# A float32 decoder trunk: where the later sums of one w_down tile are made, and one more unit in seven products

## The chip, the cores and the metric

The kernel runs on one core of one Trainium2 chip. The metric is the time of one execution on the device, in microseconds (us). Three runs of the kernel before gave 2436.99, 2437.06 and 2437.28 us; the median is 2437.06 us. The profile is of one further execution, whose own time is 2436.77 us. In it the span from the first to the last instruction is 2435.1 us.

## The reference

Two layers over 256 positions and 2048 channels, all in float32:

```
h = rms_norm(x, mix_norm[l]);  proj = h @ w_in[l]          # q, k, v, u, v of the SGU, two gates
branch_a = sliding_window_attention(q, k, v, sinks) @ w_attn_branch[l]
branch_b = chunked_sgu(gelu(uv), ...) @ w_sgu_branch[l]
merged   = sigmoid(gate_a) * branch_a + sigmoid(gate_b) * branch_b
x  = x + merged @ w_out[l]
h2 = rms_norm(x, ffn_norm[l])
x  = x + (silu(h2 @ w_gate[l]) * (h2 @ w_up[l])) @ w_down[l]   # hidden width 5632
```

The matrix products are nearly all of the work. The inner width of the feed-forward part is 11 blocks of 512.

## The kernel before, in words

**Jobs.** The program is a list of jobs (`add_job`). Each job is one matrix product: 256 positions by K inputs, times K by 1024 outputs (512 for one job of keys and values). K is cut into *units* of 512 inputs. The outputs of a job lie in PSUM banks of 128 positions by 512 outputs.

**Three matmuls for one.** A float32 matrix is split into a high part in the float32r format and the remainder, the low part. Each block product is then three matmuls with 512 columns (`three`, lines 401 to 403): high by high, high input by low weight, low input by high weight. The weights' high parts `whi` are made by ACT (line 258) and their low parts `wlo` by DVE (line 266). Both work on a *part*, 128 x 1024 numbers.

**Whole steps and products.** A unit is done in one of two ways. In the plain way it takes four *whole steps*; each uses one part and issues 12 matmuls. In the other way (`m` of the job counts the units done so) the 2 x 2 blocks of the unit are multiplied in seven *products* after Winograd's form of Strassen's method. Each product uses one part and issues 6 matmuls, so the unit takes 42 matmuls and not 48. For that, four sums of weight blocks are made by DVE (`Stream.add`, line 242), with three parts more to split, and the four sums of the input blocks must exist too. The first seven to nine products of a job follow each other without a whole step between them.

**The stream.** `Stream.fill` runs ahead of TensorE: at step s it emits the high part of step s+5, the low part of step s+4 and the weight sums that are due. `SUM_AT` gives the due step of each sum, counted from the job's first product: for `m=1` they lie 6 to 3 steps ahead of it, for `m=2` 7 ahead to 1 behind. There are five buffers for low parts, so the low part of step s+4 can be written only when step s-1 is done on TensorE. The raw weights lie in five buffers of 1 MB that the queue of SP fills.

**The input side.** A `Unit` holds 512 inputs of all positions, transposed: the high part `uh` and the low part `ul`, and, if its products need them, the sums' high and low parts `sh` and `sl`. `transposed` makes a unit: DVE transposes blocks, POOL's queue gathers them by 16 small transfers, ACT splits off the high part and DVE the low part (line 592, or line 510 in `combine`). With `sums=True` it goes on to the sums in the same go: four additions of 128 x 256 (line 522), the split by ACT (line 525) and the low part by DVE (line 510). `add_sums` makes the same sums afterwards for a unit that already exists: it first adds high and low parts again (line 605) into a tile `full`, then does the same three things.

**The order.** Every engine executes in the order in which the program emits its instructions. `after(n, fn)` emits `fn` n slots later; a whole step is one slot and a product half a slot. DVE and ACT work off everything in one row: the parts of the stream, the evictions of finished banks, the input side.

**Places in memory.** The tiles `uh`, `ul`, `sh`, `sl`, the gates, the hidden blocks, the tiles of the transposition and the sums all come from one pool of 25 places (`N_BIG`). A tile gets a place with its first write. Where none is free, the writing instruction waits until the last reader of an older tile is done, and what stands behind it on its engine waits too.

**The stretches around the change.** In the token mixer the last jobs are, in this order: the first pair of the second branch's gates, the two jobs of the first branch (2 units each, no products; `branch(ga, 0)`, then `branch(ga, 2)`), the last pair of the second branch's gates (`gate(gb, 2)`, 4 units), and the two jobs of the second branch. The feed-forward part goes in rounds over the blocks 0-3, 4-7 and 8-10. A round has gate and up jobs for two blocks at a time, with two units in seven products, and then two w_down jobs. `M_DOWN` is `((1, 2), (1, 2), (1, 1))`: in the first two rounds the first w_down job has one unit in products, and the second has two. So block fs[1] of those rounds is the "second input tile" of w_down, whose sums only the second job uses.

Of the kernel before, what the change touches and what calls it, by code (L numbers as in the profile page):

```python
# [45 lines left out]
M_OUT, M_FFN, M_DOWN = (0, 1), (2, 2, 2), ((1, 2), (1, 2), (1, 1))  # L46
UP_TWO = (0, 2, 4, 6, 8)
M_Q = 0
M_GATE, M_ATT, M_SGU = (1, 1, 1, 1), (0, 0), (1, 0)
M_V, M_U = 1, 1  # L50
SGU_SUMS = 8


@with_exitstack
def hybrid_trunk(ctx: ExitStack, tc: tile.TileContext, x, mix_norm, w_in, q_norm, k_norm, sinks,
# [37 lines left out]
    NF = FF // CW  # L93
# [16 lines left out]
    sums, uses = {}, []  # L110
# [186 lines left out]
    def after(n, fn):  # L297
        steps.append((slot_no[0] + n, fn))
# [16 lines left out]
    def evicting(c, fn, then=None, ahead=None, late_then=THEN_LATE):  # L315

        if c == 0 or job_no[0] == len(jobs):
            for t in range(NT):
                if ahead is not None:
                    ahead(t)  # L320
                soon(lambda t=t: fn(t))
            if then is not None:
                after(1, then)
        else:
            late = behind(1, *T1_LATE)
            if ahead is not None:
                ahead(0)
                after(late - 1, lambda: ahead(1))
            soon(lambda: fn(0))
            after(late, lambda: fn(1))  # L330
            if then is not None:
                after(behind(2, *late_then), then)
# [200 lines left out]
    def transposed(units, c, src, cols=None, on_pe=False, sums=False, at_once=False):  # L533

        unit = Unit(sums)

        def scaled(k):
            return 1.0 if cols is None else cols[:, k:k + 1]

        def highs(k0, n, src_t):  # L540
            step = n if cols is None else 1
            for k in range(0, n, step):
                nc.scalar.activation(unit.hi[:, k0 + k:k0 + k + step, :], src_t[:, k:k + step, :], AF.Copy,
                                     scale=scaled(k0 + k))

        def lows(k0, n, src_t):
            step = n if cols is None else 1
            for k in range(0, n, step):
                kk = slice(k0 + k, k0 + k + step)
                nc.vector.scalar_tensor_tensor(  # L550
                    out=flat(unit.lo[:, kk, :]), in0=flat(src_t[:, k:k + step, :]), scalar=scaled(k0 + k),
                    in1=flat(unit.hi[:, kk, :].bitcast(F32)), op0=ALU.mult, op1=ALU.subtract)

        def ready():
            units[c] = unit

        if on_pe:
            pts = []
            for b in range(2):
                pt = ps_at.tile([P, 2, S], F32, tag="at", name=nm("pt"))  # L560
                for kk in range(2):
                    k = 2 * b + kk
                    for t in range(NT):
                        nc.tensor.transpose(pt[:, kk, t * P:(t + 1) * P], src[:, t, k * P:(k + 1) * P], ident)
                highs(2 * b, 2, pt)
                pts.append(pt)

            def rest():
                for b in range(2):
                    lows(2 * b, 2, pts[b])  # L570
                ready()

            if at_once:
                rest()
            else:
                after(1, rest)
            return

        tt = landed()
        n = gathered(tt, src)  # L580
        tv = tt.rearrange("p i k t c -> p (k t) i c")
        def scale_all():
            if cols is not None:
                for k in range(4):
                    nc.scalar.activation(tt[:, :, k], tt[:, :, k], AF.Copy, scale=scaled(k))

        def split():
            scale_all()
            nc.scalar.activation(blocks(unit.hi), tv, AF.Copy)

        def lower():
            nc.vector.tensor_tensor(out=blocks(unit.lo), in0=tv, in1=blocks(unit.hi).bitcast(F32), op=ALU.subtract)
            ready()

        if not sums:
            after(n, split)
            after(n + 1, lower)
        else:
            after(n, scale_all)
            combine(unit, tv, n + (cols is not None), ready)  # L600
# [423 lines left out]
    for l in range(DEPTH):  # L1024

        pl = layer[l]
        parameters(pl)
        kv = slot([P, NT, CW], name="kv")
        qs = [slot([P, NT, CW], name="q") for _ in range(2)]
        att, spa = Attention(pl), Spatial(pl, norm)  # L1030

        def scaled_into(c, dst, ps):
            evicting(c, lambda t: None,
                     ahead=lambda t: nc.scalar.activation(dst[:, t, :], ps[t], AF.Copy, scale=norm.r[t]))

        def kv_done(c, ps):
            scaled_into(0, kv, ps)
            att.keys(kv)
            if l:
                att.begin()  # L1040

        def q_done(c, ps):
            scaled_into(c, qs[c], ps)
            att.queries(c, qs[c])
            if c == 1 and not l:
                att.begin()

        after(2, lambda unit=norm.units[0]: add_sums(unit))
        for done in (kv_done, q_done)[::-1 if l else 1]:
            run(norm.units, done)  # L1050
        run(norm.units, spa.v)
        run(norm.units, spa.u)

        ga, gb, mT = [None] * NCH, [None] * NCH, [None] * NCH

        def gate(dst, j):
            def done(c, ps):
                dst[j + c] = slot([P, NT, CW], name="gate")
                def tanh(t):
                    nc.scalar.activation(dst[j + c][:, t, :], ps[t], AF.Tanh, scale=norm.rh[t])  # L1060

                evicting(c, lambda t: None, ahead=tanh)
            run(norm.units, done)

        def branch(dst, j, units, then=None):
            def done(c, ps):
                d = dst[j + c]

                def then_():
                    then(j + c)  # L1070
                    transposed(mT, j + c, ga[j + c], sums=j + c == 0)

                evicting(c, lambda t: nc.vector.scalar_tensor_tensor(out=d[:, t, :], in0=d[:, t, :], scalar=1.0,  # L1073
                                                                     in1=ps[t], op0=ALU.add, op1=ALU.mult),
                         then_ if then is not None else None)
            run(units, done)

        def merge(j):
            nc.vector.tensor_tensor(out=flat(ga[j]), in0=flat(ga[j]), in1=flat(gb[j]), op=ALU.add)

        for j in (0, 2):
            gate(ga, j)
        gate(gb, 0)
        for j in (0, 2):
            branch(ga, j, att.attT)
        after(SGU_SUMS, lambda unit=spa.sguT[0]: add_sums(unit))
        gate(gb, 2)
        for j in (0, 2):
            branch(gb, j, spa.sguT, merge)

        norm = Norm(ffn_cols(l))
        residual(mT, norm, max(M_FFN), scale=0.5)

        nxt = Norm(mix_cols(l + 1)) if l + 1 < DEPTH else None
        for i, fs in enumerate(ROUNDS):
            hid, hT = {}, {}

            def gate_done(f, c, ps):
                hid[f] = a = slot([P, NT, CW], name="hid")

                evicting(c, lambda t: None,
                         ahead=lambda t: nc.scalar.activation(a[:, t, :], ps[t], AF.Silu, scale=norm.r[t]))

            def up_done(f, c, ps):
                a = hid[f]

                def upped(t):
                    nc.vector.scalar_tensor_tensor(out=a[:, t, :], in0=ps[t], scalar=norm.r[t], in1=a[:, t, :],
                                                   op0=ALU.mult, op1=ALU.mult)

                evicting(c, upped, lambda: transposed(hT, f, a, on_pe=f == NF - 1, sums=f in fs[:max(M_DOWN[i])]))

            for f in fs[::2]:
                if f + 1 < NF:
                    run(norm.units, lambda c, ps: gate_done(f + c, c, ps))
                    run(norm.units, lambda c, ps: up_done(f + c, c, ps))
                else:
                    run(norm.units, lambda c, ps: (gate_done, up_done)[c](f, c, ps))
            if i == len(ROUNDS) - 1:
                if nxt is not None:  # L1120
                    prepare(l + 1)
                residual(hT, nxt, M_Q, out if nxt is None else None)
            else:
                partial(hT)
        norm = nxt
# [37 lines left out]
```

## Time and profile before

| what | value |
|---|---|
| median of three runs | 2437.06 us |
| the profiled execution's own time | 2436.77 us |
| its span | 2435.1 us |
| TensorE (PE) busy | 2419.4 us, 99% |
| weight loads (PEld) busy | 1992.8 us, 82% |
| VectorE (DVE) busy | 2080.6 us, 85% |
| ScalarE (ACT) busy | 1488.6 us, 61% |
| GpSimd (POOL) busy | 494.2 us, 20% |
| DMA | 530.81 MB, mean 218 GB/s |

Times in rows are microseconds from the start of the span, if not marked ns. A row of a timeline gives start, duration, engine, line of the kernel, operation, the tiles written and read, the shape of the tile and how many instructions are merged into the row; in brackets stand how long the engine was idle before it and what ended the wait. A row of the stretches gives the stretch, its length, then busy time and instruction count of each engine, the granted TensorE clock, the busy share of the DMA engines and GB/s. Matmuls are pipelined and the ends of their rows are modelled, so they overlap: the distance of two starts is what a matmul costs. The count of an engine in a stretch includes what reaches in from the neighbouring stretch.

### The profile page before, as it was taken

What the parts mean: (1) busy time and instruction counts of PE and PEld (TensorE: products, weight loads), DVE (VectorE), ACT (ScalarE), POOL (GpSimd) and SP (SyncE); (2) the same over time, 40 slices, a digit from 0 to 9 for tenths busy, and PEclk for the clock granted to TensorE, in tenths of its full rate; (3) what the DMA queues carried; (4) which work ended last, traced back from release to release, by engine and by line L of the source; (5) the groups of instructions that cost most, each with busy time, mean ns of one, the idle gap of its engine ahead of it and who ended that gap; (6) DMA issues with size and microseconds to landing.
All of it is one profiled execution on the core that took longest, in us unless ns stands there. A gap on an engine that the chain in (4) does not pass through costs nothing.

```text
span 2435.1 us, 30941 instructions
## 1 busy us (share of the span) xinstructions
PE 2419.4 (99%) x10866; PEld 1992.8 (82%) x10866; DVE 2080.6 (85%) x2271; ACT 1488.6 (61%) x1828; POOL 494.2 (20%) x919
## 2 busy tenths in 40 slices
PE   9999999999999999999999999999999999999999
PEld 7888888888888887888888888888887888788887
DVE  7898768788988899889879977687789888988896
ACT  6566546466666666575666655554667566656663
POOL 1421300541220022002235123004402200220020
PEclk9999999999999999999999999999999999999999
DMA  8655556776576657666776555567855766476664
GB/s 309 202 191 186 180 180 223 227 261 227 185 259 199 245 196 242 211 223 225 263 248 230 193 169 189 185 207 220 291 209 192 257 188 258 162 268 189 250 209 171
DMA packets 174701, 530.81 MB, mean 218 GB/s; under 512 B 23617, under 2 KB 26289, under 8 KB 174545
## 3 DMA queue, kind: packets, MB, share of 16 engines
q1 hardware_dynamic: 142128, 491.73, 58.3%
q0 software_dynamic: 32096, 36.83, 5.9%
q8 instruction: 85, 1.39, 0.2%
q14 instruction: 72, 0.58, 0.1%
q10 hardware_dynamic: 320, 0.27, 0.0%
HBM read 483.66 MB, written 16.78 MB: 206 GB/s over the span
## 4 chain that ended last, share of the span: by engine, by line
PE 93%; DVE 3%; ACT 2%; DMA 1%; issue 1%; POOL 0%; DVEq 0%; ACTq 0%
PE acc L401 30%; PE acc L402 30%; PE acc L403 30%; DVE wlo L266 1%; ACT whi L258 1%; DMA tt<-blk 1%; PE po L891 1%; PE psc L849 1%; DVE sum L242 1%; PE ppt L880 0%; DMA raw<-in_w_in_dram 0%; PE psg L958 0%; DVE sums L522 0%; ACT acc L437 0%; DVE raw L242 0%
## 5 line engine op out<-in xcount | busy, mean ns | idle before, releaser
L266 DVE TENSOR_TENSOR wlo<-raw,whi 128x1024 fp32r<-128x1024 f32 (+1 forms) x970 | 1161.2, 1220 | 252.0 <-PE acc L402 145.3
L258 ACT ACTIVATE whi<-raw 128x1024 fp32r<-128x1024 f32 (+1 forms) x970 | 1007.9, 1056 | 569.7 <-PE acc L403 486.7
L401 PE MATMUL acc<-whi,uh 128*128 128x512 f32 x2864 | 1121.5, 392 | 1.9 <-DVE gate L1073 1.5
L402 PE MATMUL acc<-wlo,uh 128*128 128x512 f32 x2864 | 1115.2, 389 | 3.4 <-DVE wlo L266 3.4
L403 PE MATMUL acc<-whi,ul 128*128 128x512 f32 x2864 | 1115.1, 389 | 0.3 <-DVE ul L550 0.2
L491 POOL DMA_DIRECT2D tt<-blk x800 | 392.3, 498 | 1388.2 <-issue 331.2
L401 PEld LDWEIGHTS acc<-whi,uh 128*128 128x128 f32 x2864 | 537.6, 188 | 116.8 <-issue 2.3
L402 PEld LDWEIGHTS acc<-wlo,uh 128*128 128x128 f32 x2864 | 537.7, 188 | 115.6 <-DVE wlo L266 5.8
L403 PEld LDWEIGHTS acc<-whi,ul 128*128 128x128 f32 x2864 | 537.6, 188 | 113.7 <-DVE ul L550 0.6
L258 ACT ACTIVATE whi<-sum 128x1024 fp32r<-128x1024 f32 x144 | 152.4, 1058 | 123.9 <-PE acc L403 103.3
L402 PE MATMUL acc<-wlo,sh 128*128 128x512 f32 x576 | 224.9, 390 | 1.8 <-DVE wlo L266 1.8
L401 PE MATMUL acc<-whi,sh 128*128 128x512 f32 x576 | 225.4, 391 | 0.9 <-ACT acc L437 0.5
L403 PE MATMUL acc<-whi,sl 128*128 128x512 f32 x576 | 224.3, 389 | 0.0
L266 DVE TENSOR_TENSOR wlo<-sum,whi 128x1024 fp32r<-128x1024 f32 x144 | 175.1, 1219 | 19.6 <-PE acc L402 18.1
L401 PEld LDWEIGHTS acc<-whi,sh 128*128 128x128 f32 x576 | 108.1, 188 | 27.4 <-ACT acc L437 5.4
L402 PEld LDWEIGHTS acc<-wlo,sh 128*128 128x128 f32 x576 | 108.1, 188 | 26.5 <-DVE wlo L266 4.2
L403 PEld LDWEIGHTS acc<-whi,sl 128*128 128x128 f32 x576 | 108.1, 188 | 22.5
L437 ACT ACTIVATE acc<-acc 128x512 f32<-128x512 f32 x144 | 84.6, 587 | 23.2 <-PE acc L403 21.9
L242 DVE TENSOR_TENSOR raw<-raw,sum 128x1024 f32<-128x1024 f32 x72 | 88.2, 1225 | 2.5
L242 DVE TENSOR_TENSOR sum<-raw 128x1024 f32<-128x1024 f32 x72 | 87.9, 1220 | 1.9 <-DMA raw<-in_w_gate_dram 1.5
L242 DVE TENSOR_TENSOR sum<-raw,raw 128x1024 f32<-128x1024 f32 x72 | 88.0, 1222 | 0.8
L242 DVE TENSOR_TENSOR raw<-raw,raw 128x1024 f32<-128x1024 f32 x72 | 87.8, 1220 | 0.6 <-DMA raw<-in_w_gate_dram 0.5
(128 smaller groups left out, 1050.7 us busy)
## 6 DMA issues: line engine op xcount, KB each, us to landing
raw<-in_w_in_dram SPq DMA_DIRECT2D x112, 1024.0 KB, 5.5
raw<-in_w_down_dram SPq DMA_DIRECT2D x88, 1024.0 KB, 7.0
raw<-in_w_gate_dram SPq DMA_DIRECT2D x80, 1024.0 KB, 7.0
raw<-in_w_up_dram SPq DMA_DIRECT2D x80, 1024.0 KB, 6.8
raw<-in_w_out_dram SPq DMA_DIRECT2D x32, 1024.0 KB, 6.6
tt<-blk POOLq DMA_DIRECT2D x800, 32.0 KB, 4.6
raw<-in_w_attn_branch_dram SPq DMA_DIRECT2D x16, 1024.0 KB, 5.8
raw<-in_w_sgu_branch_dram SPq DMA_DIRECT2D x16, 1024.0 KB, 5.6
```

Of the source, the lines that this page charges most:

```text
L242: nc.vector.tensor_tensor(out=self.raw(dst), in0=self.raw(one), in1=self.raw(two), op=ALU.subtract)
L258: nc.scalar.activation(hi[:, k, :], raw[:, k, :], AF.Copy)
L266: nc.vector.tensor_tensor(out=lo[:, k, :], in0=raw[:, k, :], in1=hi[:, k, :].bitcast(F32), op=ALU.subtract)
L401: nc.tensor.matmul(ps, a, hi, start=first, stop=False, skip_group_check=True)
L402: nc.tensor.matmul(ps, a, lo, start=False, stop=False, skip_group_check=True)
L403: nc.tensor.matmul(ps, b, hi, start=False, stop=last, skip_group_check=True)
L437: nc.scalar.activation({"11": x, "t2": e, "t3": y}[name], a, AF.Copy)
L491: nc.gpsimd.dma_start(blocks(d)[:, :, i] if whole else d[:, i].rearrange("p k t c -> p (k t) c"), src)
L849: nc.tensor.matmul(pscore[:, i, :nk], self.qT[pair // 4][j * HD:(j + 1) * HD, pair % 4, t * P:(t + 1) * P], self.kT[j * HD:(j + 1) * HD, : ...
L891: nc.tensor.matmul(p[:, h, :], pT[kb][:, h, :], self.kv[:, kb, KVW + g * HD:KVW + (g + 1) * HD], start=kb == 0, stop=kb == t)
```

## The change

Two things are changed, each in both layers.

First, block fs[1] of the first two feed-forward rounds is transposed without sums. Its sums are made by `add_sums`, emitted five slots after the first w_down job of the round begins. Before, they were emitted right behind the unit's own split.

Second, the last pair of the second branch's gates has two units in seven products and not one. So the sums of the second unit of h are needed there; `add_sums` makes them, emitted two slots after the second job of the first branch begins. The sums of the SGU's first tile are emitted 9 slots after the gate job's begin and no longer 8.

```
-M_GATE, M_ATT, M_SGU = (1, 1, 1, 1), (0, 0), (1, 0)
+M_GATE, M_ATT, M_SGU = (1, 1, 1, 2), (0, 0), (1, 0)
 M_V, M_U = 1, 1
-SGU_SUMS = 8
+SGU_SUMS, SUMS_LATE, SECOND_SUMS = 9, 5, 2
...
         for j in (0, 2):
+            if j:
+                after(SECOND_SUMS, lambda unit=norm.units[1]: add_sums(unit))
             branch(ga, j, att.attT)
         after(SGU_SUMS, lambda unit=spa.sguT[0]: add_sums(unit))
         gate(gb, 2)
...
-                evicting(c, upped, lambda: transposed(hT, f, a, on_pe=f == NF - 1, sums=f in fs[:max(M_DOWN[i])]))
+                evicting(c, upped, lambda: transposed(hT, f, a, on_pe=f == NF - 1, sums=f == fs[0]))
...
+            if M_DOWN[i][1] > 1:
+                after(SUMS_LATE, lambda hT=hT, f=fs[1]: add_sums(hT[f]))
             if i == len(ROUNDS) - 1:
```

## The prediction, made before the changed kernel had run

> **What bounds the kernel now.** I read the page first, then who TensorE waited for, then the stretches of the jobs concerned, then the rows of DVE in them.
>
> ```profile
> span 2435.1 us, 30941 instructions
> PE 2419.4 (99%) x10866; PEld 1992.8 (82%) x10866; DVE 2080.6 (85%) x2271; ACT 1488.6 (61%) x1828; POOL 494.2 (20%) x919
> ...
> PE acc L402 <- DVE wlo L266: 5.1, 10, 0.6
> ```
>
> TensorE sets the time, and what it visibly waits for is DVE's low parts: ten times, 5.1 us. The next rows are stretches, each from the first matmul of a job to that of the next. In this order: the first up job of round one, its second gate job, its second up job; the second up job of round two; the same two of layer 1; the two w_down jobs of round one; the second job of the first branch; the last gate job.
>
> ```profile
> 579.08:619.88 40.80, 40.80 (x182) 33.78 (x180) 38.06 (x36) 25.33 (x27) 1.06 (x3) 1.00 0.62 232
> 619.88:660.68 40.80, 40.80 (x182) 33.78 (x180) 40.70 (x42) 28.76 (x31) 14.62 (x30) 1.00 0.67 233
> 660.68:703.68 43.00, 41.76 (x181) 33.42 (x180) 41.15 (x42) 26.57 (x29) 1.10 (x3) 1.00 0.55 196
> 909.37:952.36 42.99, 41.80 (x182) 33.43 (x181) 41.17 (x42) 26.55 (x29) 1.04 (x3) 1.00 0.55 196
> 1869.10:1912.10 43.00, 41.79 (x182) 33.49 (x181) 41.09 (x42) 26.55 (x29) 1.10 (x3) 1.00 0.54 196
> 2117.77:2160.76 42.99, 41.78 (x181) 33.44 (x181) 41.17 (x42) 26.56 (x29) 1.06 (x3) 1.00 0.55 196
> 703.68:745.84 42.16, 42.16 (x187) 34.91 (x186) 35.53 (x33) 24.78 (x27) 15.85 (x31) 1.00 0.75 233
> 745.84:787.04 41.20, 41.12 (x182) 33.70 (x180) 36.34 (x32) 26.31 (x30) 2.41 (x2) 1.00 0.72 231
> 342.69:364.44 21.75, 21.75 (x97) 18.02 (x96) 16.92 (x16) 8.52 (x8) 0.00 (x0) 1.00 0.39 142
> 364.44:406.60 42.16, 42.16 (x187) 34.91 (x186) 33.48 (x33) 23.81 (x26) 0.00 (x0) 1.00 0.60 200
> ...
> ```
>
> A job with two units in products has 180 matmuls. Undisturbed it takes 40.80 us, so a matmul costs 40.80 / 180 = 0.2267 us; a product of 6 costs 1.36 us, a whole step of 12 costs 2.72 us. The second up job of rounds one and two takes 43.00, 42.99, 43.00 and 42.99 us. It loses 2.20 + 2.19 + 2.20 + 2.19 = **8.78 us** in all, and ahead of it DVE is full (40.70 of 40.80 us). The second w_down job loses 41.20 - 40.80 = 0.40 us. The jobs of the mixer lose nothing: 186 x 0.2267 = 42.16 us.
>
> [...]
>
> **Part one: the later sums.** These are TensorE's waits in the first of the four jobs, and DVE's and ACT's rows around them.
>
> ```profile
> 667.48 0.39 PE L401 MATMUL acc<-whi,sh 128*128 128x512 f32 x1
> 668.34 0.50 PE L402 MATMUL acc<-wlo,sh 128*128 128x512 f32 x1 [0.47 <-DVE wlo L266]
> ...
> 670.61 0.50 PE L402 MATMUL acc<-wlo,uh 128*128 128x512 f32 x1 [0.61 <-DVE wlo L266]
> ...
> 672.20 0.50 PE L401 MATMUL acc<-whi,sh 128*128 128x512 f32 x1 [0.16 <-ACT acc L437]
> ```
> ```profile
> 664.46 1.22 DVE L242 TENSOR_TENSOR sum<-raw,raw 128x1024 f32<-128x1024 f32 x1
> 665.60 0.42 DVE L522 TENSOR_TENSOR sums<-tt 128x256 f32<-128x256 f32 x1
> ...
> 667.06 1.22 DVE L266 TENSOR_TENSOR wlo<-raw,whi 128x1024 fp32r<-128x1024 f32 x1
> 668.20 1.22 DVE L242 TENSOR_TENSOR sum<-raw,raw 128x1024 f32<-128x1024 f32 x1
> 669.33 3.49 DVE L266 TENSOR_TENSOR wlo<-raw,whi 128x1024 fp32r<-128x1024 f32 x3
> 672.74 1.23 DVE L510 TENSOR_TENSOR sl<-sums,sh 128x1024 fp32r<-128x1024 f32 x1
> 673.87 5.76 DVE L266 TENSOR_TENSOR wlo<-raw,whi 128x1024 fp32r<-128x1024 f32 x5
> ```
> ```profile
> 667.18 1.06 ACT L525 ACTIVATE sh<-sums 128x1024 fp32r<-128x1024 f32 x1 [1.98 <-DVE sums L522]
> ```
>
> The removed work stands exactly there. The four sums hold DVE from 665.60 to 667.06, that is 1.46 us, and the low part of the sums another 673.87 - 672.74 = 1.13 us. A 128 x 1024 operation counts 1.14 us in a full row (667.06, 668.20, 669.33). Without them the low part that came at 667.06 starts at 665.60 and ends at 666.82. TensorE wants it at 667.71: the product starts at 667.48, its second matmul 0.23 later. So the first wait is gone. The weight sum follows at 666.74, the next low part at 667.87 to 669.09; it is wanted at 667.71 + 1.36 = 669.07. That is a touch late, 0.02 plus the hand-over. The three low parts behind it end at 670.2, 671.4 and 672.5, and are wanted at 670.4, 671.8 and 673.2: in time, since the 1.13 us are gone too. ACT's 0.16 us wait goes with the 1.98 us that ACT stood for the sums. By their starts the three waits lose 668.34 - 667.71 = 0.63, then 670.61 - 668.34 - 1.36 = 0.91, then 672.20 - 670.61 - 5 x 0.2267 = 0.46 us; that makes 2.00, so the restarts add 0.20, 0.07 each. I keep **0.15 us** of each 2.20: the 0.02, a hand-over and a restart. The bounds are 0 and, if the second wait stays whole, 1.1 us (0.91 and what it drags along). The gain is 8.78 - 0.6 = **8.2 us**.
>
> Where the sums go, in the first w_down job five slots after its start, there is this.
>
> ```profile
> 718.67 1.23 DVE L266 TENSOR_TENSOR wlo<-raw,whi 128x1024 fp32r<-128x1024 f32 x1 [0.68 <-issue]
> ...
> 721.39 1.23 DVE L266 TENSOR_TENSOR wlo<-raw,whi 128x1024 fp32r<-128x1024 f32 x1 [0.36 <-issue]
> 724.12 1.23 DVE L266 TENSOR_TENSOR wlo<-raw,whi 128x1024 fp32r<-128x1024 f32 x1 [1.50 <-PE acc L402]
> 726.83 1.22 DVE L266 TENSOR_TENSOR wlo<-raw,whi 128x1024 fp32r<-128x1024 f32 x1 [1.49 <-PE acc L402]
> ```
> ```profile
> L605 DVE TENSOR_TENSOR full<-uh,ul 128x1024 f32<-128x1024 f32 x4 | 4.8, 1212 | 0.0
> ```
>
> DVE waits for TensorE there, so it is as far ahead as five buffers allow: four whole steps, 10.9 us less the part's own 1.22. `full` (1.21), the sums (1.46) and their low part (1.14) add 3.8 us; the idle of these four rows is 4.0. Taken away, that cover would still leave some 9 us of lead, so the price is **0**. ACT's one more split moves there and has room (24.78 of 42.16 us busy). No DMA is added or moved.
>
> **Part two: two units in products.** It saves 6 matmuls a layer: 6 x 0.2267 = **1.36 us**. On DVE it adds three low parts and four weight sums (7 x 1.14 = 8.0 us) and `add_sums` (1.14 + 1.46 + 1.14 = 3.7 us). Six of eight weight sums, and all of `add_sums`, fall into the stretch 342.69 to 364.44, which has 21.75 - 16.92 = 4.8 us idle on DVE.
>
> ```profile
> 343.86 1.28 DVE L1073 SCALAR_TENSOR_TENSOR gate<-gate,acc 128x512 f32<-128x512 f32 x2
> 345.44 1.22 DVE L266 TENSOR_TENSOR wlo<-raw,whi 128x1024 fp32r<-128x1024 f32 x1 [0.30 <-issue]
> 348.15 1.23 DVE L266 TENSOR_TENSOR wlo<-raw,whi 128x1024 fp32r<-128x1024 f32 x1 [1.50 <-PE acc L402]
> ...
> 353.11 0.39 PE L402 MATMUL acc<-wlo,uh 128*128 128x512 f32 x1
> ...
> 747.78 0.60 ACT L979 ACTIVATE y<-acc 128x512 f32<-128x512 f32 x1 [3.40 <-DMA kept<-y]
> 748.28 1.05 ACT L258 ACTIVATE whi<-raw 128x1024 fp32r<-128x1024 f32 x1
> ```
>
> A wait is added that no row shows: a place in the pool of 25. At 345 these tiles live, counted in the code: h's four units 8, the first one's sums 2, six gates, the attention's two units 4, the SGU's two units 4. That is 24. `full` takes the last place; the tile of the sums needs one more, and the first to fall free is the attention's first unit, read last at 353.11 + 0.39 = 353.5. That a full pool stops an engine is seen at 747.78: ACT waits 3.40 us for a transfer out of the place it needs, and the weight part behind it starts only then. [...]
>
> DVE's order is then, with 1.14 per large operation, 0.6 per eviction, 0.12 more for each of the two weight sums that overwrite a block just read (my estimate from other rows of this kind):
>
> ```
> 345.44 low part; weight sum 346.6; full 347.7; low part 348.9; weight sum 350.0
> 351.1 four sums: wait for the place until 353.6; done 355.1
> 355.1 low, sum 356.2; low 357.3, sum 358.5; low part of the sums 359.7
> 360.9 low (2nd product), sum; 363.2 low (3rd), two evictions; 365.6 low (4th), sum
> 367.8 low (5th), sum, eviction; 370.7 low (6th), sum; 373.0 low (7th) ends 374.2; 8th 375.4; 9th 376.5
> ```
>
> The first product starts at 364.44, so the 6th low part is wanted at 364.44 + 5 x 1.36 + 0.23 = 371.47 and is there at 371.9; the 7th is wanted at 372.83 and there at 374.2. The 8th and 9th are wanted at 374.19 and 375.55, which the stall then covers. So TensorE stalls 1.4 and a restart, **1.5 us** a layer, and part two nets 2 x (1.5 - 1.36) = **+0.3 us**. The bounds are no stall (-2.7 us for both layers) and twice the stall (+3.3). I take the list's value. Behind the waiting sums stand the low parts, and for those TensorE; on ACT the split of the sums waits until 355.1, with its own weight parts far ahead. SP's loads of raw weights that wait for these low parts come later with them; they feed units two further on, so I price them at 0. The SGU's sums fall nearer to their use; my list, carried on, still leaves them over 4 us.
>
> **Sum.** -8.2 + 0 + 0.3 = -7.9 us against the profiled span of 2435.1, so a span of 2427.2 and an execution of 2436.77 - 7.9 = 2428.9 us. The median of the runs lies 0.29 above the profiled one: **2429.2 us**.
>
> **Rivals.** *(a) No wait for a place*: one more place is free than I count. Then DVE's list runs 2.5 us earlier, the 7th low part is there at 371.7 for 372.83, and part two brings its 2.7 us: 2437.06 - 8.2 - 2.7 = 2426.2. For it: DVE has 4.8 us idle there. Against: the count. *(b) Half the stall stays*: the second wait of the up jobs (0.61) was only 0.02 us from staying in my list; if it stays whole, 1.1 us of each 2.2 is left: 2437.06 - 4.4 + 0.3 = 2433.0. *(c) The pool is fuller than I count by one*: `full` waits itself until 353.5, and the low part of the sums waits for the attention's second unit, in use until the stretch ends at 364.44. DVE's list is then 4.8 us later, TensorE stalls 6.3 us a layer: -8.2 + 2 x (6.3 - 1.36) = +1.7, so 2438.8, slower than before. It decides once a layer's stall passes 1.36 + 8.2 / 2 = 5.5 us. Against it: in the w_down job 24 tiles and one y fit, so 25 really are there. *(d) Nothing moves*: the up jobs are slow for DVE's load as a whole, and another of its operations takes the freed 1.46 us: 2437 us. Against: all rows after 664 are accounted for.
>
> **How the numbers follow.** Forecast 0.60, (a) 0.20, (b) 0.12, (c) 0.05, (d) 0.03. The forecast's own spread is about 1.5 us (0.3 per stall). The range takes in (a) and reaches into (b): 2425.6 to 2432.8. A measurement of this kernel tells about 0.2%, 4.9 us, from no change, so faster means below 2432.2: the forecast, (a) and a part of (b), 0.85. Same is the rest of (b), (c) and (d) as priced, 0.13; slower, (c) with a worse price, 0.02.
>
> **What would show it.** Right: the second up jobs of rounds one and two take 40.8 to 41.1 us; no sums<-tt row stands in them and a sums<-full row stands in the w_down job, which stays at 42.16; the sums in the first branch's second job start when TensorE ends that job's fourth step, after about 2.5 us of idle; the gate job, 180 matmuls, takes 42.2 to 42.5 and not 40.8. Wrong: waits on a low part at the head of w_down, a gate job over 43.5, or an up job still over 42.

## The result and the profile after

Nine runs of the changed kernel have a median of 2430.19 us (2427.61 to 2431.75), nine of the kernel before 2437.06 us (2434.88 to 2439.11). The ratio is 0.9969, with a 95% interval of 0.9961 to 0.9978: **faster by 0.31%**. The forecast was 2429.2 us, with a range of 2425.6 to 2432.8. The profiled execution took 2430.19 us, with a span of 2428.5.

From the page of the changed kernel, and its list of what TensorE waited for:

```profile
span 2428.5 us, 30953 instructions
PE 2414.4 (99%) x10854; PEld 1991.0 (82%) x10854; DVE 2104.0 (87%) x2301; ACT 1501.3 (62%) x1836; POOL 496.4 (20%) x919
...
PE acc L402 <- DVE wlo L266: 3.6, 8, 0.6
...
PE acc L401 <- ACT acc L437: 1.2, 1, 1.2
```

TensorE has 12 matmuls less, six a layer, and DVE 30 operations and 23 us more. The next rows are stretches of the changed kernel, each one job: the first branch's second job; the last gate job; the second up job and the first w_down job of round one; the second up job of round two; then, of layer 1, the gate job and the second up jobs of rounds one and two. The columns are stretch, length, then busy time and count of PE, PEld, DVE, ACT and POOL, the granted clock, DMA share and GB/s.

```profile
341.60:363.36 21.76, 21.76 (x97) 18.02 (x96) 18.99 (x21) 9.35 (x9) 0.00 (x0) 1.00 0.42 142
363.36:405.72 42.36, 41.43 (x182) 33.57 (x180) 41.60 (x42) 27.35 (x29) 0.00 (x0) 1.00 0.55 199
660.00:702.14 42.14, 41.39 (x181) 33.63 (x180) 39.80 (x38) 26.17 (x28) 1.09 (x3) 1.00 0.56 200
702.14:744.30 42.16, 42.16 (x187) 34.92 (x186) 39.05 (x39) 25.66 (x28) 15.90 (x31) 1.00 0.77 234
907.95:948.93 40.98, 40.98 (x182) 33.72 (x180) 38.64 (x37) 25.94 (x28) 1.10 (x3) 1.00 0.56 206
1568.32:1610.64 42.32, 41.39 (x181) 33.55 (x180) 41.59 (x42) 27.36 (x29) 0.00 (x0) 1.00 0.55 199
1864.68:1906.04 41.36, 41.12 (x182) 33.72 (x181) 39.01 (x37) 26.05 (x28) 1.10 (x3) 1.00 0.56 204
2111.75:2152.76 41.01, 41.01 (x181) 33.71 (x180) 38.67 (x37) 25.94 (x28) 1.10 (x3) 1.00 0.57 206
```

The four second up jobs take 42.14, 40.98, 41.36 and 41.01 us, where they took 43.00, 42.99, 43.00 and 42.99: 165.49 against 171.98, a gain of **6.5 us**. The w_down job, which took in the moved sums, stays at 42.16. The two gate jobs take 42.36 and 42.32 us where they took 42.16, although each has six matmuls less: **0.36 us lost**. That makes -6.1 us. The spans differ by 6.6 us; the other 0.5 is the net of jobs that the change does not touch, and these scatter by more than that: one of them alone took 1.4 us longer in this execution (last section).

These are DVE's rows in the changed kernel ahead of the gate job:

```profile
346.63 1.22 DVE L605 TENSOR_TENSOR full<-uh,ul 128x1024 f32<-128x1024 f32 x1
347.77 1.22 DVE L266 TENSOR_TENSOR wlo<-raw,whi 128x1024 fp32r<-128x1024 f32 x1
348.90 1.22 DVE L242 TENSOR_TENSOR raw<-raw,raw 128x1024 f32<-128x1024 f32 x1
352.46 0.42 DVE L522 TENSOR_TENSOR sums<-full 128x256 f32<-128x256 f32 x1 [2.34 <-PE acc L402]
...
353.93 1.22 DVE L266 TENSOR_TENSOR wlo<-raw,whi 128x1024 fp32r<-128x1024 f32 x1
...
369.59 1.22 DVE L266 TENSOR_TENSOR wlo<-raw,whi 128x1024 fp32r<-128x1024 f32 x1
370.73 1.22 DVE L242 TENSOR_TENSOR sum<-raw,raw 128x1024 f32<-128x1024 f32 x1
371.86 4.63 DVE L266 TENSOR_TENSOR wlo<-raw,whi 128x1024 fp32r<-128x1024 f32 x4
```

And TensorE's waits at the head of that job:

```profile
370.87 0.50 PE L402 MATMUL acc<-wlo,sh 128*128 128x512 f32 x1 [0.32 <-DVE wlo L266]
...
373.14 0.50 PE L402 MATMUL acc<-wlo,uh 128*128 128x512 f32 x1 [0.62 <-DVE wlo L266]
```

DVE stands idle for 2.34 us ahead of the first of the four sums, released by TensorE: this is the wait for a place in the pool. The first of them reads only `full`, which DVE had written itself, so TensorE can hold it up only through the place that it is written to. And 352.46 is where the job's fourth step ends (341.60 + 4 x 2.72 = 352.48), as forecast. The 6th and the 7th low part (369.59 and 371.86) come late, and TensorE waits for them in the two PE rows. The same group of sums in layer 1 waits as well, for 2.34 us, ahead of the row at 1557.41. The row of all sums on `full` shows 4.7 us of idle time in all, put down to TensorE, and 2.34 of it is the wait above:

```profile
L522 DVE TENSOR_TENSOR sums<-full 128x256 f32<-128x256 f32 x20 | 8.4, 420 | 4.7 <-PE acc L402 4.7
```

### The profile page after: what moved, and what is told of

Its sections match the earlier page's. It is cut to its first block, busy times and chain, and to the rows that moved or that the text cites. A ratio compares the mean times of both kernels' runs of the same rounds, so it can differ in the third digit from the quotient of the medians.

```text
span 2428.5 us, 30953 instructions
## 1 busy us (share of the span) xinstructions
PE 2414.4 (99%) x10854; PEld 1991.0 (82%) x10854; DVE 2104.0 (87%) x2301; ACT 1501.3 (62%) x1836; POOL 496.4 (20%) x919
## 4 chain that ended last, share of the span: by engine, by line
PE 96%; DVE 1%; issue 1%; ACT 1%; DMA 1%; POOL 0%; DVEq 0%; ACTq 0%; POOLq 0%
PE acc L401 31%; PE acc L402 31%; PE acc L403 31%; PE po L891 1%; DVE wlo L266 1%; ACT whi L258 1%; PE psc L849 1%; PE ppt L880 0%; PE psg L958 0%; DMA kept<-y 0%; DMA tt<-blk 0%; PE pt L564 0%; POOL tt L491 0%; PE pwarm L379 0%; ACT acc L437 0%
## 5 line engine op out<-in xcount | busy, mean ns | idle before, releaser
L401 PE MATMUL acc<-whi,sh 128*128 128x512 f32 x592 | 231.2, 390 | 1.5 <-ACT acc L437 1.2
L402 PE MATMUL acc<-wlo,sh 128*128 128x512 f32 x592 | 230.8, 390 | 0.8 <-DVE wlo L266 0.6
L403 PE MATMUL acc<-whi,sl 128*128 128x512 f32 x592 | 230.5, 389 | 0.0
L266 DVE TENSOR_TENSOR wlo<-sum,whi 128x1024 fp32r<-128x1024 f32 x148 | 180.0, 1220 | 19.0 <-PE acc L402 18.1
```

What stands on the lines that cost most here:

```text
L266: nc.vector.tensor_tensor(out=lo[:, k, :], in0=raw[:, k, :], in1=hi[:, k, :].bitcast(F32), op=ALU.subtract)
L401: nc.tensor.matmul(ps, a, hi, start=first, stop=False, skip_group_check=True)
L402: nc.tensor.matmul(ps, a, lo, start=False, stop=False, skip_group_check=True)
L403: nc.tensor.matmul(ps, b, hi, start=False, stop=last, skip_group_check=True)
```

## The experiments

All times are medians. The kernel before ran beside them on the same chips: 2437.79 us in the first group of four, 2437.75 in the second.

| run | us | ratio to before, 95% interval | gate jobs | second up jobs of round one | of round two |
|---|---|---|---|---|---|
| only_late_sums | 2428.57 | 0.9964 (0.9952 to 0.9977) | 42.16, 42.16 | 42.16, 41.00 | 40.98, 40.95 |
| only_two_units | 2437.83 | 1.0002 (0.9993 to 1.0011) | 42.35, 42.40 | 44.19, 43.00 | 42.99, 42.94 |
| changed_again | 2429.82 | 0.9965 (0.9952 to 0.9979) | 42.36, 42.35 | 41.30, 41.74 | 41.00, 40.96 |
| sums_one_slot_later | 2426.71 | 0.9957 (0.9944 to 0.9969) | 40.80, 40.80 | 41.48, 42.16 | 40.96, 40.96 |
| sums_two_slots_later | 2429.08, one run | | 40.84, 40.85 | 42.20, 40.97 | 40.97, 41.01 |
| w_down_sums_at_head | 2431.19, one run | | 42.35, 42.32 | 42.17, 40.97 | 40.97, 40.97 |
| first_sums_moved_too | 2424.16 | 0.9945 (0.9932 to 0.9957) | 40.80, 40.80 | 40.80, 40.80 | 40.80, 40.80 |
| one_slot_later_again | 2426.46 | 0.9958 (0.9945 to 0.9972) | 40.80, 40.80 | 41.55, 40.98 | 41.01, 40.97 |

### Each part alone

Both edits are shown against the changed kernel. Part one alone takes the gate job's part back:

```
-M_GATE, M_ATT, M_SGU = (1, 1, 1, 2), (0, 0), (1, 0)
+M_GATE, M_ATT, M_SGU = (1, 1, 1, 1), (0, 0), (1, 0)
-SGU_SUMS, SUMS_LATE, SECOND_SUMS = 9, 5, 2
+SGU_SUMS, SUMS_LATE = 8, 5
-            if j:
-                after(SECOND_SUMS, lambda unit=norm.units[1]: add_sums(unit))
```

> Part one alone: the sums of the second w_down input tile are made in the w_down job; the last gate job has one unit in products as before. Theory (the four second up jobs are the whole gain, part two is worth nothing): the four jobs fall from 43.0 us to between 40.9 and 42.1 each, the last gate job is 42.16, the time is 6.5 to 8.2 us below before, as far below as with both parts. Rival (part two brings its six matmuls a layer and part one less): 4 to 5 us below before.

Part two alone leaves the w_down sums where they were:

```
-... sums=f == fs[0]))
+... sums=f in fs[:max(M_DOWN[i])]))
-            if M_DOWN[i][1] > 1:
-                after(SUMS_LATE, lambda hT=hT, f=fs[1]: add_sums(hT[f]))
```

> Part two alone: the last gate job has two units in products, its input sums are emitted two slots into the first branch's second job; the w_down sums stay where they were. Theory (a place in the pool is waited for, and the stall eats the six matmuls): DVE idle about 2.3 us ahead of the first of the four sums, a gate job of 42.3 us, up jobs of 43.0, the time +0.3 us, not to be told from before. Rival (the gate part is the gain): 2.7 us below before.

Part one alone is 9.2 us below before. That is the whole gain and a little more than expected, with an interval of 5.6 to 11.7 us. Part two alone changes nothing (1.0002). In its profile the wait and the loss are the same as with both parts. From DVE's rows, and the stretch of the gate job:

```profile
353.59 0.42 DVE L522 TENSOR_TENSOR sums<-full 128x256 f32<-128x256 f32 x1 [2.33 <-PE acc L402]
```
```profile
364.50:406.85 42.35, 41.43 (x181) 33.56 (x180) 41.59 (x42) 27.30 (x29) 0.00 (x0) 1.00 0.55 199
...
661.42:705.61 44.19, 41.80 (x182) 33.42 (x180) 42.29 (x43) 26.55 (x29) 1.10 (x3) 1.00 0.53 191
```

One number was not expected: an up job of 44.19 us, 1.2 more than any of the four in the profile before. The next run takes that up.

### The changed kernel again, and what is left of the stalls

The kernel is unaltered.

> The changed kernel itself, unaltered, for comparison on the same chip and for a second profile. Theory (what is left of the stalls in the second up jobs, 1.3, 0.2, 0.6 and 0.2 us in the first profile, comes from transfers that land earlier or later from run to run and put DVE behind ahead of a stretch in which it cannot catch up): the four remainders come out in another order, each between 0.1 and 1.4 us, and where one is large DVE's low parts were already later at the head of the job before. Rival (something of the change sits in the first up job pair of layer 0): the first of the four is again 1.3 us and the others as they were.

The remainders came out in another order, 0.50, 0.20, 0.94 and 0.16 us over 40.80. Those of round two hardly move, 0.15 to 0.21 us in each of the seven profiles that have part one and leave the first input tile's sums where they were; those of round one scatter. For round one's 14 second up jobs in these seven profiles I took, from the rows of DVE and PE, how long before the job's first product its low part was ready (the lead), and set the job's length beside it. In the changed kernel's first profile, for instance, this low part is ready at 654.44 + 1.22 = 655.66 and the job starts at 660.00, a lead of 4.34:

```profile
654.44 1.22 DVE L266 TENSOR_TENSOR wlo<-raw,whi 128x1024 fp32r<-128x1024 f32 x1
```

| lead at the head, us | 5.51 | 5.18 | 5.14 | 5.04 | 4.92 | 4.75 | 4.34 | 4.33 | 4.32 | 4.31 | 4.30 |
|---|---|---|---|---|---|---|---|---|---|---|---|
| length, us | 40.97 to 41.00 (4 jobs) | 41.30 | 41.36 | 41.48 | 41.55 | 41.74 | 42.14 | 42.16 | 42.20 | 42.17 | 42.16 |

All 14 lie on one line to 0.05 us: 40.97, and a microsecond for each microsecond that the lead lacks to 5.51. The leads of round two are 5.51 and 5.52. With a lead of 4.31 and the sums still in place the job takes 44.19 us (part two alone). DVE's lateness there is thus paid in full. In the changed kernel's profile DVE loses the lead in these waits; the profile before has none at this place:

```profile
603.46 1.22 DVE L242 TENSOR_TENSOR sum<-raw 128x1024 f32<-128x1024 f32 x1 [0.80 <-DMA raw<-in_w_gate_dram]
...
606.67 1.23 DVE L242 TENSOR_TENSOR raw<-raw,raw 128x1024 f32<-128x1024 f32 x1 [0.86 <-DMA raw<-in_w_gate_dram]
```

Two loads of w_gate come too late for DVE, and from there on it has no idle time in which to catch up. The other jobs agree: ahead of the ten that took 41.3 us or more DVE waits 0.45 to 1.97 us for loads of w_gate, and ahead of the four at 41.00 or less it does not.

These two loads are late because they were issued late, and not because they took longer. They took 10.5 and 12.6 us from issue to landing, against 10.4 and 13.2 in the profile before; but the first was issued 660.00 - 592.90 = 67.10 us ahead of the up job, and in the profile before 660.68 - 591.76 = 68.92. SP issues a load when DVE's low parts have freed the buffer, as its waits in the kernel before show (total, times, longest):

```profile
SPq L222 <- DVE wlo L266: 1956.2, 404, 19.4
```

And DVE had lost time earlier. The rows of ACT, DVE and SP, of the changed kernel and then of the kernel before:

```profile
563.57 1.72 ACT L585 ACTIVATE tt<-tt,vcols 128x256 f32<-128x256 f32 x4 [5.28 <-DMA tt<-blk]
566.42 1.23 DVE L592 TENSOR_TENSOR ul<-tt,uh 128x1024 fp32r<-128x1024 f32 x1 [2.75 <-ACT uh L589]
592.90 16.54 SPq L222 DMA_DIRECT2D raw<-in_w_gate_dram  x5
```
```profile
561.83 1.71 ACT L585 ACTIVATE tt<-tt,vcols 128x256 f32<-128x256 f32 x4 [3.25 <-DMA tt<-blk]
564.66 1.23 DVE L592 TENSOR_TENSOR ul<-tt,uh 128x1024 fp32r<-128x1024 f32 x1 [2.23 <-ACT uh L589]
591.76 17.22 SPq L222 DMA_DIRECT2D raw<-in_w_gate_dram  x5
```

ACT waits for the gathers of a unit of h2, and DVE for ACT. DVE's row `ul` begins 93.58 us ahead of the up job, where it began 96.02 ahead in the profile before. So in this profile the chain goes back to these gathers. In 16 of round one's 20 second up jobs over all ten profiles, the second load is issued 27.6 us after this row `ul`; in the other four, where `ul` comes earliest, 67.8 us ahead of the job. Not all of the lateness comes this way: ahead of three jobs the load that DVE waits for was issued as early as in the profile before and took 8.9 to 9.2 us, not 8.6. Why the gathers land when they do is not shown, and no run moved them or made a load late on purpose: all this is read from the traces and not tried. It also stays open whether the change has a share in it. In layer 0 every profile of an altered kernel has a wait for w_gate at this place, with part one alone as with part two alone; of the kernel before there is one profile, and it has none.

### Is it the wait for the place?

```
-SGU_SUMS, SUMS_LATE, SECOND_SUMS = 9, 5, 2
+SGU_SUMS, SUMS_LATE, SECOND_SUMS = 9, 5, 3
```

> The changed kernel, but the sums of the second unit of h are emitted three slots into the first branch's second job, not two. Theory (DVE stands idle for a place that falls free with that job's fourth step): the first of the four sums comes just as the place falls free, one low part and one weight sum go ahead of it that before stood behind it, 2.3 us of DVE's time; the 7th low part of the gate job is then in time, the gate job takes 40.8 us and the time is 2.7 to 3.1 us below the changed kernel. Rival (DVE has too much work there whatever the order): emitted later the sums only make the lead smaller, the gate job stays at 42.3 us or grows, and the time is the changed kernel's or up to 1 us more.

DVE's rows of this run:

```profile
350.58 1.22 DVE L605 TENSOR_TENSOR full<-uh,ul 128x1024 f32<-128x1024 f32 x1
351.71 1.22 DVE L266 TENSOR_TENSOR wlo<-raw,whi 128x1024 fp32r<-128x1024 f32 x1
352.85 1.22 DVE L242 TENSOR_TENSOR sum<-raw 128x1024 f32<-128x1024 f32 x1
353.98 0.42 DVE L522 TENSOR_TENSOR sums<-full 128x256 f32<-128x256 f32 x1
...
371.12 4.62 DVE L266 TENSOR_TENSOR wlo<-raw,whi 128x1024 fp32r<-128x1024 f32 x4
```

A low part and a weight sum (351.71, 352.85) now stand ahead of the sums, and the sums start without a wait. In the changed kernel this low part was emitted behind the sums, and DVE did not take it up while it stood idle for 2.34 us: it began at 353.93, behind the four sums, 363.36 - 353.93 = 9.43 us ahead of the gate job; here it begins 364.59 - 351.71 = 12.88 us ahead of it. The 7th low part comes 371.12 - 364.59 = 6.53 us after the job's start, where it came 371.86 - 363.36 = 8.50 after it; the stretch of the job:

```profile
364.59:405.39 40.80, 40.80 (x182) 33.78 (x180) 39.70 (x40) 27.01 (x29) 0.00 (x0) 1.00 0.58 206
```

DVE does the same work, emitted later, and the six matmuls of each layer come through: 42.36 to 40.80 us. The time is 3.1 us below the changed kernel on the same chip (2429.82 to 2426.71), as the theory had it. No run gave the pool a 26th place. The repetition beside the last run gave 2426.46 us and the gate jobs 40.80 again.

> The kernel with the sums one slot later, unaltered, on the same chip as the run before it. Theory (the second up jobs of round two lose 0.16 us in every execution, those of round one 0.17 us plus what the lead lacks to 5.5): gate jobs 40.8 us, up jobs of round two 40.96, those of round one between 40.96 and 42.2 and on that line; the time about 10.5 us below before. Rival (the gain of the first run was the chip's or the run's): less than 9 us below before.

Here the up jobs are 41.55 and 40.98 us in round one and 41.01 and 40.97 in round two, on the line above. The time is 11.3 us below before.

One slot more:

```
-SGU_SUMS, SUMS_LATE, SECOND_SUMS = 9, 5, 3
+SGU_SUMS, SUMS_LATE, SECOND_SUMS = 9, 5, 4
```

> As the run with the sums one slot later, but by two slots: emitted four slots into the first branch's second job. Theory (only the wait for the place cost time; with one slot it is gone, so a second slot has nothing more to bring): no wait ahead of the sums, and since they now stand behind one more low part and weight sum, DVE is idle some 1.1 us earlier in the job; the 7th low part of the gate job comes about 1 us later than with one slot, just in time, and the job takes 40.8 to 41.1 us. Rival (each slot later helps, since DVE's load is spread): 40.8 us with a larger lead than with one slot.

The gate jobs take 40.84 and 40.85 us. DVE's lead at the 7th low part is 0.18 us there and 0.64 with one slot (from the same two kinds of rows). So later is not better by itself: once the wait is gone, a further slot only takes lead. The stretch of the gate job:

```profile
364.91:405.75 40.84, 40.84 (x181) 33.69 (x180) 40.10 (x40) 27.08 (x29) 0.00 (x0) 1.00 0.58 206
```

### The cover of the moved sums

```
-SGU_SUMS, SUMS_LATE, SECOND_SUMS = 9, 5, 2
+SGU_SUMS, SUMS_LATE, SECOND_SUMS = 9, 1, 2
```

> The changed kernel, but the later sums of the second w_down tile are emitted one slot into the w_down job and not five. This takes their cover away: in the first profile the low parts there are 4 us ahead, not 9. Theory (they are hidden by the lead of the low parts, and cost the lead what they take): of the 4 us lead 2.4 to 2.7 go, the least lead is 1.3 to 1.6 us, the first w_down job stays at 42.16 us. Rival (there is no cover but idle time): the w_down job grows by 1 to 3 us.

```profile
703.27:745.43 42.16, 42.16 (x188) 34.91 (x187) 38.70 (x39) 25.54 (x28) 15.86 (x31) 1.00 0.77 232
```

The w_down job stays at 42.16 us: the lead hides the sums even at the head. These are DVE's rows there:

```profile
705.11 1.22 DVE L266 TENSOR_TENSOR wlo<-raw,whi 128x1024 fp32r<-128x1024 f32 x1
706.25 1.22 DVE L605 TENSOR_TENSOR full<-uh,ul 128x1024 f32<-128x1024 f32 x1
...
711.78 2.36 DVE L266 TENSOR_TENSOR wlo<-raw,whi 128x1024 fp32r<-128x1024 f32 x2
```

The least lead fell from 3.96 to 2.74 us and not to 1.3 to 1.6. What the sums take was forecast rightly, but the expectation took it from the wrong part. The low part at 705.11 had the least lead, 3.96; it stands ahead of `full` and keeps it. The first of the two at 711.78 stands behind `full` and the four sums. It is wanted after seven products and a whole step, at 703.27 + 7 x 1.36 + 2.72 + 0.23 = 715.74, and is ready at 713.00; its lead fell by 2.43 us, from 5.17 in the first profile to 2.74. (In this job six products follow each other at the head and the seventh comes after a whole step; with two units it is ten, and not seven to nine as said of the kernel before.)

### Taking the rest of the stall away

This run starts from the kernel with the sums one slot later, and moves the first input tile's sums as well.

```
-SGU_SUMS, SUMS_LATE, SECOND_SUMS = 9, 5, 3
+SGU_SUMS, SUMS_LATE, SECOND_SUMS, FIRST_LATE = 9, 5, 3, 8
...
-... sums=f == fs[0]))
+... sums=f == fs[0] and M_DOWN[i][1] == 1))
...
+                    if f == fs[2] and M_DOWN[i][1] > 1:
+                        after(FIRST_LATE, lambda hT=hT, f=fs[0]: add_sums(hT[f]))
                     run(norm.units, lambda c, ps: up_done(f + c, c, ps))
```

> The kernel with the sums one slot later in the mixer, and with the sums of the first w_down input tile moved as well: they leave the second gate job and are made eight slots into the second up job, by the way that adds high and low parts again. Theory (the remainders of the stalls, 0.17 us and as much as DVE's lead at the head of the second up job is under 5.5 us, are DVE's lateness alone): 2.6 us less of DVE's work ahead of the stall bring the lead to about 8 us, the four second up jobs take 40.8 us each, the first w_down job stays at 42.16 with a least lead near 1.5 us, the time is 1 to 2.4 us below the kernel with the sums one slot later. Rival (DVE is as full behind the stall as ahead of it): the stall moves into the head of the w_down job and the time stays or grows by up to 2 us.

The stretches of round one's second up and first w_down job, and of round two's second up job:

```profile
658.31:699.11 40.80, 40.80 (x181) 33.78 (x180) 40.51 (x42) 27.07 (x30) 0.40 (x1) 1.00 0.57 207
699.11:741.27 42.16, 42.16 (x187) 34.91 (x186) 39.19 (x40) 25.75 (x28) 16.55 (x33) 1.00 0.75 232
904.74:945.54 40.80, 40.80 (x182) 33.78 (x180) 40.14 (x41) 26.66 (x30) 0.41 (x1) 1.00 0.58 206
```

All four up jobs take 40.80 us, with DVE busy for 40.1 to 40.5 of them. The lead at their head is 8.11 us in round two, and 6.92 and 7.88 in round one: the loads were late here too, and it no longer matters. The time is 2424.16 us, 2.3 below the kernel with the sums one slot later on the same chip, and this is the fastest version: 0.9945 of the kernel before. The four up jobs account for 1.3 of the 2.3 us (164.51 to 163.20 between the two profiles); the rest is not accounted for. I had the lead in the w_down job wrong again: 3.68 us and not 1.5. I had counted what the moved sums take there, and not the 2.6 us that they give ahead of it.

## Why the prediction was right, point by point

**What bounds the kernel**: right. The four second up jobs held nearly all that could be gained, and DVE's low parts were what TensorE waited for.

**Part one's gain**: right in its mechanism, and the size was 8.2 us against 6.5 in the profile. The term that was mis-sized is the 0.15 us kept of each stall. It measured 0.18 and 0.21 us in round two, as worked out from the rows. In round one it measured 1.34 and 0.56 us: the prediction took DVE's row of one execution as fixed, but in the execution measured DVE came to these two jobs with 1.17 and 0.37 us less lead than 5.51. The prediction itself had found that the next low part was a touch late (0.02 us). So there was nothing in hand, and each microsecond of lateness had to be paid. By the prediction's own signs these two jobs speak against it: it had named 40.8 to 41.1 us as right and an up job over 42 as wrong, and they took 41.36 and 42.14.

**The cover in the w_down job**: right, 42.16 us before and after, and still so when the sums were put at the head.

**Part two**: right in mechanism and size. The wait for a place was forecast at 351.1 to 353.6, 2.5 us, and measured 2.34. The gate job began 1.08 us earlier than before (363.36 against 364.44). With that shift the forecast starts are 352.5 for the sums, 369.6 for the 6th low part and 371.9 for the 7th; measured were 352.46, 369.59 and 371.86. The net loss was forecast at 0.15 us a layer and measured 0.20 and 0.16.

**The rivals**: (a), no wait, fell with the rows of the wait, and its price was right: with the wait gone by emitting the sums a slot later, the gate jobs take the 40.80 us it gave. (b), half the stall stays, held in one job of four. There the second wait stayed whole, 0.62 us, as (b) had it; what tipped it was DVE's lateness of 1.17 us. (c), a fuller pool, and (d), nothing moves, did not come.

**The sum**: -7.9 us forecast. The change measured -6.9 us by its first nine runs and -8.0 by the five beside the experiments. That the total came so near is in part luck. In the profiled execution the stretches that were forecast give -6.1 us, 1.8 less than forecast, and jobs that the change does not touch made up 0.5 of it.

## What to carry to other kernels

When work is moved in an engine's row, count what it must find at its new place: time, and a free buffer. Here a wait of 2.34 us for a buffer in each layer held DVE's low parts behind it and ate the 12 saved matmuls (gate jobs of 42.36 and 42.32 us), and emitting the same work one slot later, when the buffer falls free, brought them back (40.80 us). DVE was full over a long stretch here, busy for 40.70 of 40.80 us in the job ahead of the stall in the profile before. Removing just enough to clear the stall left the time to what made DVE late: round one's second up jobs took 40.97 to 42.20 us in seven profiles. With 2.6 us less work ahead of the stall all four second up jobs took 40.80 us.

## What the runs showed of the hardware that was not expected

In two profiles of one unaltered program the same gathers took different times to land, the slowest 8.1 us in one and 6.0 in the other, and one of TensorE's jobs at that place took 33.63 and 32.17 us. It is the first w_down job of the last round in layer 1: 33.63 us in the changed kernel's first profile, 32.17 in its second, and 32.19 in the profile before. ACT's and TensorE's rows in the changed kernel's first profile:

```profile
2359.07 1.06 ACT L589 ACTIVATE uh<-tt 128x1024 fp32r<-128x1024 f32 x1 [2.65 <-issue]
```
```profile
2362.56 0.50 PE L401 MATMUL acc<-whi,sh 128*128 128x512 f32 x1 [1.16 <-ACT acc L437]
```

ACT's row at the same place in its second profile, and then in the kernel before:

```profile
2358.33 1.06 ACT L589 ACTIVATE uh<-tt 128x1024 fp32r<-128x1024 f32 x1
```
```profile
2365.64 1.06 ACT L589 ACTIVATE uh<-tt 128x1024 fp32r<-128x1024 f32 x1 [1.22 <-issue]
```

ACT waits 2.65 us ahead of the gathered tile `tt` in the first, not at all in the second, and 1.22 us in the kernel before. The timeline names no releaser there ("issue"), but the tile's own summaries, over the 16 gathers that fill it, show one (minimum, median and maximum). In the same order:

```profile
DMA to landing us min/median/max: 2.8/5.6/8.1
```
```profile
DMA to landing us min/median/max: 2.1/5.0/6.0
```
```profile
DMA to landing us min/median/max: 2.0/5.7/6.8
```

The slowest gather took 8.1, 6.0 and 6.8 us. In the first and the third of these profiles it is the last one issued, at 2350.8 and 2358.7, so it landed at 2358.9 and 2365.5, 0.1 to 0.2 us ahead of ACT's row. The copies behind it in ACT's row come later, and TensorE waits 1.16 us for one of them in the first. That the gather is the cause is inferred from these numbers; it was not tried. Over the ten profiles this job took between 32.17 and 34.29 us. The change does not touch it.
